# The MLP on h times g_mlp with its norm's row factor applied to h around it, block 0's gate behind its MLP, and h of two blocks kept on chip

## The chip, the cores and the metric

The kernel runs on one core of one Trainium2 chip. The metric is the device time of one execution in microseconds (us). Five engines work side by side, each through its own instructions in order: TensorE (PE, matrix products; its weight loads are listed as PEld), VectorE (DVE), ScalarE (ACT), GpSimd (POOL) and SyncE (SP, whose queue issues all DMA transfers of this kernel). Tiles lie in on-chip memory (SBUF), 128 partitions wide; products land in PSUM.

## The reference

One step of a one-layer encoder over 2048 prompt frames and 32 frames of a second, cached stream, 2080 rows of 1024 channels. Cut to what the change touches:

```python
def rmsnorm(x, g, eps=EPS):
    y = x * lax.rsqrt(jnp.mean(x * x, axis=-1, keepdims=True) + eps)
    return y * g

hp = hp + merge(oa, ob, ...)            # attention outputs @ w_out, residual

def ffn_ple(h, p, g_mlp, w_up, w_down, w_ple_gate, w_ple_proj):
    c = rmsnorm(h, g_mlp)
    h = h + jnp.square(jax.nn.relu(c @ w_up)) @ w_down
    return h + jax.nn.sigmoid(h @ w_ple_gate) * (p @ w_ple_proj)

y = rmsnorm(hp, g_final)
```

w_up is 1024 x 4096, w_down 4096 x 1024, w_ple_gate 1024 x 1024, w_ple_proj 256 x 1024. Before the merge stand two attention groups, A (differential, over all earlier chunks) and B (a band).

With r the factor 1/sqrt(mean(h*h) + eps) of a row and v = 1/(r*r), a squared relu lets r*r be taken out: the square of relu(r * x) is r*r times the square of relu(x). So h + MLP(r*h*g) equals r*r * (h*v + MLP(h*g)). The kernel after computes it in this second form.

## The kernel before, in words

**Tiling.** Channels lie on the partitions and rows along the free axis. The 2080 rows are cut into four blocks of 512, 512, 512 and 544 (`BN`); block 3's products are made in two pieces of 272 (`SUBS`). Every float32 operand of a product is split into a rounded high part and the rest: ACT writes the high part, POOL or DVE subtracts it (`split`), and `mm3` makes three products per term: high x high, high x low, low x high. `wunit` loads 512 KB of weights (ring `wr` of two), ACT makes `wh` and POOL makes `wl` (rings of three).

**Order.** The program is written as stages, but a planner orders each engine's instructions: it runs the program on a timeline of its own and takes, of the instructions that are ready there, the one that stands earliest in the program. So a later stage fills the gaps of an earlier one. On the chip the order of each engine is then fixed, and an engine that waits holds everything behind it.

**The stages that matter here**, as `run` writes them: attention A of the late rows (`JA1`); outproj(0) and outproj(1) with the loads and norms of the attention outputs (`oload`); the MLP of block 0, alone, then of block 1, alone; gate(1) and final(1); then outproj(2), outproj(3), gate(0), the norms of blocks 2 and 3, and one MLP for both of them; gate(2), final(2), gate(3), final(3). `outproj` adds x to the product, collects the sum of squares of h on POOL (`sq`) and writes h to `hS` in device memory. `colnorm` sums `sq` over the partitions with two products by a matrix of ones and makes r with ACT and DVE, which goes to `rS`. `cnorm` reads h and r back, multiplies by g_mlp and r on DVE and splits the result into cH and cL. The MLP then reads h a second time (`hload`) and adds the down product of each chunk to it on DVE. `mlp` runs 16 chunks of 256 hidden channels; `mlp_up` of a chunk comes before `mlp_down` of the chunk before.

**Block 0's gate** comes late: its h is written back to `hS` after its MLP, and read again for gate(0) behind outproj(3).

**Rings and memory.** In the first part the MLPs and gate(1) share two PSUM buffers (`mm`, MM = 2), because attention holds the other six; afterwards these six become `md`, used by outproj(2), outproj(3), gate and the down products. `actq` has two buffers: a block's cH and cL, then gate's hH and hL. `hq` has one buffer for h, `uq` a ring of eight for the MLP's, gate's and final's working tiles. In the second part `acth` has four buffers and `hh` two. The pools `wk` and `fk` (working tiles: `tmp` a ring of four, `r` and `acc` of two) are opened twice, for the first and for the second part. A pool opened over freed memory waits, tile by tile, for those who used it.

The lines to know: L149 and L153 are `split`, L168 to L170 the three products of `mm3`, L838 to L844 outproj's add and squares, L859 cnorm's multiply, L880 to L890 the norm factor, L914 relu, L949 the add of a down product to h, L993 to L1014 the gate, L1031 to L1054 final.

## Time and profile before

| | us |
|---|---|
| median of 3 runs | 3315.77 |
| lowest, highest | 3314.72, 3323.53 |
| the profiled execution | 3310.69 |
| its span, first to last instruction | 3308.8 |
| TensorE busy | 3096.1 |
| mean granted TensorE clock | 0.975 |

Where the stages lie in the profiled execution, from the first and last starts of their tiles: outproj(0) begins at 932.5; the MLPs of blocks 0 and 1 run from 1073 to 2154, beside attention, whose last row goes out at 2210; gate(1) starts at 2154; outproj(2) and (3) lie between 2219 and 2339; gate(0) between 2339 and 2405; the MLP of blocks 2 and 3 from 2406 to 3165; then the last two gates.

How to read it: a page gives the busy time of each engine, then groups of instructions by source line, with `out<-in` by the names of the tiles, a count, busy time and mean time of one. An idle stretch of an engine is put down to what ended it. Matmuls are pipelined: each is listed with its own length, but the next starts before it ends, so the distance from start to start is what a matmul costs. A busy-time table by stretch gives for each engine the busy us and, in brackets, the instructions.

### The profile page before, as it was taken

What the parts mean: (1) busy time and instruction counts of PE and PEld (TensorE: products, weight loads), DVE (VectorE), ACT (ScalarE), POOL (GpSimd) and SP (SyncE); (2) the same over time, 40 slices, a digit from 0 to 9 for tenths busy, and PEclk for the clock granted to TensorE, in tenths of its full rate; (3) what the DMA queues carried; (4) which work ended last, traced back from release to release, by engine and by line L of the source; (5) the groups of instructions that cost most, each with busy time, mean ns of one, the idle gap of its engine ahead of it and who ended that gap; (6) DMA issues with size and microseconds to landing.
All of it is one profiled execution on the core that took longest, in us unless ns stands there. A gap on an engine that the chain in (4) does not pass through costs nothing. (4 is left out here: it accounts for less than half of the span.)

```text
span 3308.8 us, 50118 instructions
## 1 busy us (share of the span) xinstructions
PE 3096.1 (94%) x17881; PEld 2710.5 (82%) x17881; DVE 1669.4 (50%) x3952; ACT 1698.4 (51%) x3717; POOL 1468.8 (44%) x1083
## 2 busy tenths in 40 slices
PE   6988989999989999999899999989889999999998
PEld 6877778889977888777777877877779999999987
DVE  6117777454555545476765656656442232223335
ACT  4226666566665766666665656654442222222245
POOL 4335654432334433444544444565753333333365
PEclk9999899999999999999999999999999999999999
DMA  7488777686788654545655345347631111111123
GB/s 232 159 252 244 205 217 205 204 247 195 215 235 215 180 145 134 155 132 138 200 136 136 112 132 144 116 146 226 178 105 52 45 46 50 46 45 45 53 86 101
DMA packets 519073, 488.93 MB, mean 148 GB/s; under 512 B 37884, under 2 KB 414016, under 8 KB 518824
## 3 DMA queue, kind: packets, MB, share of 16 engines
q1 hardware_dynamic: 518824, 485.73, 50.8%
q8 instruction: 142, 2.33, 0.3%
q14 instruction: 107, 0.88, 0.1%
HBM read 379.06 MB, written 110.49 MB: 148 GB/s over the span
## 5 line engine op out<-in xcount | busy, mean ns | idle before, releaser
L153 POOL TENSOR_TENSOR wl<-wr,wh 128x1024 fp32r<-128x1024 f32 x338 | 820.0, 2427 | 1026.3 <-ACT wh L149 983.4
L949 DVE TENSOR_TENSOR h<-h,dps 128x512 f32<-128x512 f32 (+1 forms) x640 | 373.1, 585 | 584.6 <-PE dps L170 572.2
L149 ACT ACTIVATE wh<-wr 128x1024 fp32r<-128x1024 f32 x338 | 356.9, 1056 | 563.9 <-PE dps L169 278.4
L168 PE MATMUL dps<-uh,wh 128*128 128x512 f32 (+1 forms) x1280 | 459.7, 359 | 22.0 <-DVE h L949 16.7
L168 PE MATMUL ups<-cH,wh 128*128 128x512 f32 (+1 forms) x1280 | 452.0, 353 | 8.2 <-ACT relu L914 8.0
L170 PE MATMUL dps<-uh,wl 128*128 128x512 f32 (+1 forms) x1280 | 451.7, 353 | 0.0
L169 PE MATMUL ups<-cL,wh 128*128 128x512 f32 (+1 forms) x1280 | 451.5, 353 | 0.0
L169 PE MATMUL dps<-ul,wh 128*128 128x512 f32 (+1 forms) x1280 | 451.4, 353 | 0.0
L170 PE MATMUL ups<-cH,wl 128*128 128x512 f32 (+1 forms) x1280 | 451.0, 352 | 0.0
L168 PEld LDWEIGHTS dps<-uh,wh 128*128 128x128 f32 x1280 | 242.8, 190 | 57.0 <-DVE h L949 22.8
L168 PEld LDWEIGHTS ups<-cH,wh 128*128 128x128 f32 x1280 | 241.4, 189 | 40.9 <-ACT relu L914 8.6
L170 PEld LDWEIGHTS dps<-uh,wl 128*128 128x128 f32 x1280 | 241.7, 189 | 33.0
L169 PEld LDWEIGHTS ups<-cL,wh 128*128 128x128 f32 x1280 | 241.9, 189 | 31.1 <-DVE cL L153 0.4
L170 PEld LDWEIGHTS ups<-cH,wl 128*128 128x128 f32 x1280 | 241.7, 189 | 30.1
L153 POOL TENSOR_TENSOR ul<-relu,uh 128x272 fp32r<-128x272 f32 (+1 forms) x160 | 174.9, 1093 | 205.2 <-ACT uh L149 203.8
L169 PEld LDWEIGHTS dps<-ul,wh 128*128 128x128 f32 x1280 | 242.4, 189 | 26.3
L168 PE MATMUL qps<-aH,wh 128*128 128x512 f32 (+1 forms) x640 | 231.5, 362 | 6.8 <-ACT wh L149 3.4
L545 PE MATMUL s<-ka,q 128*128 128x256 f32 (+4 forms) x784 | 192.7, 348 | 40.8 <-issue 15.7
L169 PE MATMUL qps<-aL,wh 128*128 128x512 f32 (+1 forms) x640 | 229.8, 359 | 0.0
L170 PE MATMUL qps<-aH,wl 128*128 128x512 f32 (+1 forms) x640 | 229.3, 358 | 0.0
L559 ACT ACTIVATE e<-s,nm 128x512 f32<-128x512 f32 (+3 forms) x256 | 155.1, 610 | 94.7 <-DVE nm L551 70.9
L545 PEld LDWEIGHTS s<-ka,q 128*128 128x128 f32 (+1 forms) x784 | 135.7, 195 | 66.4 <-issue 27.9
(217 smaller groups left out, 7056.9 us busy)
## 6 DMA issues: line engine op xcount, KB each, us to landing
wr<-w_up SPq DMA_DIRECT2D x96, 512.0 KB, 4.2
wr<-w_down SPq DMA_DIRECT2D x96, 512.0 KB, 3.7
wr<-w_in SPq DMA_DIRECT2D x74, 512.0 KB, 5.2
q<-qS SPq DMA_DIRECT2D x256, 128.0 KB, 4.3
v<-vSa SPq DMA_DIRECT2D x64, 512.0 KB, 3.8
ka<-kS SPq DMA_DIRECT2D x32, 512.0 KB, 7.9
wr<-w_out SPq DMA_DIRECT2D x32, 512.0 KB, 5.0
wr<-w_ple_gate SPq DMA_DIRECT2D x32, 512.0 KB, 4.4
```

What stands on the lines that cost most here:

```text
L149: nc.scalar.activation(hi, raw, AF.Copy)
L153: eng.tensor_tensor(lo, raw, hi.bitcast(F32), op=ALU.subtract)
L168: nc.tensor.matmul(ps, lh, rh, start=start and i == 0, stop=False)
L169: nc.tensor.matmul(ps, lh, rl, start=False, stop=False)
L170: nc.tensor.matmul(ps, ll, rh, start=False, stop=stop and i == n - 1)
L545: nc.tensor.matmul(s, q[:, m, hl, P * qi : P * qi + nr], kt[:, m, k0 : k0 + n], start=hl == 0, stop=hl == 1)
L559: nc.scalar.activation(dst, src, AF.Exp, bias=nmx, accum_out=z[:nr, m, bi : bi + 1])
L949: nc.vector.tensor_tensor(hv, hv, ps, op=ALU.add)
```

## The change

Four things, in the order of the program.

1. The norm's factor no longer goes into the MLP's input. `split_g` makes cH and cL from h in two instructions: ACT scales by g_mlp while it rounds, DVE multiplies by g_mlp and subtracts. `msnorm` takes the place of `colnorm`: it makes v (the mean square plus EPS) and 1/v, and writes both to device memory (`vS[2]`, `rS`). `mlp` loads v behind its first up chunk and POOL multiplies h by it, eight instructions per block; in the last down chunk each add to h is followed by a DVE multiply by 1/v.
2. gate and final of block 0 come right behind its MLP, as those of block 1 did; block 0's h is no longer written back and read again, and gate(0) and final(0) are gone from the second part.
3. Of blocks 2 and 3 h is made in place: both tiles of `hh` exist before outproj(2), outproj reads x into them and adds there, and h is not written to `hS`. Block 2's cH and cL are made inside outproj(2); block 3's (`csplit`) behind outproj(3). The MLP takes the tiles as they are.
4. `wk` and `fk` are opened once, ahead of the attention of the late rows, and stay.

```diff
-        self.vS = [self.dram([KC, D], F32, "vSa"), self.dram([KC, D], F32, "vSb")]
+        self.vS = [self.dram([KC, D], F32, "vSa"), self.dram([KC, D], F32, "vSb"), self.dram([P, T], F32, "vSm")]
...
+    def split_g(self, k, src, n, c):
+        nc = self.nc
+        g = self.g_mlp[:, k : k + 1]
+        hi, lo = c[0][:, k, :n], c[1][:, k, :n]
+        nc.scalar.activation(hi, src, AF.Copy, scale=g)
+        nc.vector.scalar_tensor_tensor(lo, src, g, hi.bitcast(F32), op0=ALU.mult, op1=ALU.subtract)
...
-            h = wk.tile([P, BLK], F32, tag="tmp", bufs=4, name="hd")[:, :n]
+            if hfull is None:
+                h = wk.tile([P, BLK], F32, tag="tmp", bufs=4, name="hd")[:, :n]
+            else:
+                h = hfull[:, d, :n]
             self.dma(h, self.xT[:, d, t0 : t0 + n])
...
-            self.dma(self.hS[:, d, t0 : t0 + n], h)
+            if hfull is None:
+                self.dma(self.hS[:, d, t0 : t0 + n], h)
+            if c is not None:
+                self.split_g(d, h, n, c)
             yield
 
-    def cnorm(self, b, wk, act, out):
+    def csplit(self, b, wk, act, out, hfull=None):
...
-        r = wk.tile([P, BLK], F32, tag="r", bufs=2, name="rl")[:, :n]
-        self.dma(r, self.rS[:, t0 : t0 + n])
         for k in range(8):
-            tmp = wk.tile([P, BLK], F32, tag="tmp", bufs=4, name="tmp")[:, :n]
-            self.dma(tmp, self.hS[:, k, t0 : t0 + n])
-            nc.vector.scalar_tensor_tensor(
-                tmp, tmp, self.g_mlp[:, k : k + 1], r, op0=ALU.mult, op1=ALU.mult
-            )
-            self.split(cH[:, k, :n], cL[:, k, :n], tmp, "act", "dve" if k % 2 else "pool")
+            if hfull is None:
+                tmp = wk.tile([P, BLK], F32, tag="tmp", bufs=4, name="tmp")[:, :n]
+                self.dma(tmp, self.hS[:, k, t0 : t0 + n])
+            else:
+                tmp = hfull[:, k, :n]
+            self.split_g(k, tmp, n, (cH, cL))
             yield
...
+    def msnorm(self, sq, b, wk, ps):
...
+            nc.scalar.activation(v, ss, AF.Copy, scale=1.0 / D, bias=EPS)
+            nc.scalar.activation(y, v, AF.Ln)
+            nc.scalar.activation(y, y, AF.Exp, scale=-1.0)
+            nc.vector.tensor_tensor(z, v, y, op=ALU.mult)
+            nc.vector.tensor_scalar(z, z, -1.0, 2.0, op0=ALU.mult, op1=ALU.add)
+            nc.vector.tensor_tensor(y, y, z, op=ALU.mult)
+        self.dma(self.vS[2][:, t0 : t0 + n], sq)
+        self.dma(self.rS[:, t0 : t0 + n], r)
...
+    def hscale(self, blocks, st, wk, src, name):
+        out = {}
+        for b in blocks:
+            out[b] = wk.tile([P, BLK], F32, tag="r", bufs=2, name=name)
+            self.dma(out[b][:, : BN[b]], src[:, 512 * b : 512 * b + BN[b]])
+        return out
...
                         nc.vector.tensor_tensor(hv, hv, ps, op=ALU.add)
+                        if rt is not None:
+                            nc.vector.tensor_tensor(hv, hv, rt[b][:, s0 : s0 + sn], op=ALU.mult)
...
-            if prev is not None:
+            if prev is None:
+                vt = self.hscale(blocks, st, wk, self.vS[2], "vt")
+                for d in range(8):
+                    for b in blocks:
+                        hv = st[b][0][:, d, : BN[b]]
+                        nc.gpsimd.tensor_tensor(hv, hv, vt[b][:, : BN[b]], op=ALU.mult)
+            else:
                 self.mlp_down(ch - 1, nf, blocks, prev, st, wk, md)
             prev = us
-        self.mlp_down(ch, nf, blocks, prev, st, wk, md)
+        self.mlp_down(ch, nf, blocks, prev, st, wk, md, self.hscale(blocks, st, wk, self.rS, "rt"))
...
             s12.close()
             self.small = False
+            wk = opened(top, "wk", 1)
+            fk = opened(top, "fk", 1)
             sq_ = ExitStack()
...
                 if b == 1:
-                    drain(self.cnorm(1, wk, actq, cn))
+                    drain(self.csplit(1, wk, actq, cn))
...
-                if b == 0:
-                    self.dma(self.hS[:, :, 512 * b : 512 * b + 512], h)
-            drain(self.gate(1, h, uq, actq, mm))
-            drain(self.final(1, h, uq, fk, mm))
+                drain(self.gate(b, h, uq, actq, mm))
+                drain(self.final(b, h, uq, fk, mm))
...
-            weave(self.outproj(2, wk, oa[2], md, acc[2]), self.oload(3, wk, act, oa), 1, 0, OW)
-            g = self.outproj(3, wk, oa[3], md, acc[3])
+            hb = {b: hh.tile([P, 8, BLK], F32, tag="h", name="h") for b in HALVES[1]}
+            g = self.oload(3, wk, act, oa)
             next(g)
-            self.colnorm(acc[2][0], 2, 1.0 / D, wk, mm, "mm", self.rS)
+            cn[2] = [act.tile([P, 8, BLK], F32R, tag="act", name=n) for n in ("cH2", "cL2")]
+            weave(self.outproj(2, wk, oa[2], md, acc[2], hb[2], cn[2]), g, 1, 0, OW)
+            g = self.outproj(3, wk, oa[3], md, acc[3], hb[3])
+            next(g)
+            self.msnorm(acc[2][0], 2, wk, mm)
             drain(g)
-            h = hload(hh, BLK, 0)
-            g = self.gate(0, h, up, act, md)
-            next(g)
-            self.colnorm(acc[3][0], 3, 1.0 / D, wk, mm, "mm", self.rS)
-            drain(g)
-            for b in HALVES[1]:
-                drain(self.cnorm(b, wk, act, cn))
-            f = self.final(0, h, up, fk, mm)
-            st = {b: (hload(hh, BLK, b),) + cn[b] for b in HALVES[1]}
+            drain(self.csplit(3, wk, act, cn, hb[3]))
+            st = {b: (hb[b],) + tuple(cn[b]) for b in HALVES[1]}
             m = self.mlp(HALVES[1], st, wk, up, mm, md)
             next(m)
-            drain(f)
+            self.msnorm(acc[3][0], 3, wk, mm)
             drain(m)
```

More of the change, by code (lines that the diff above doesn't have):

```diff
@@ L853, in cnorm @@
         out[b] = (cH, cL)
-        r = wk.tile([P, BLK], F32, tag="r", bufs=2, name="rl")[:, :n]
-        self.dma(r, self.rS[:, t0 : t0 + n])
         for k in range(8):
-            tmp = wk.tile([P, BLK], F32, tag="tmp", bufs=4, name="tmp")[:, :n]
-            self.dma(tmp, self.hS[:, k, t0 : t0 + n])
-            nc.vector.scalar_tensor_tensor(
-                tmp, tmp, self.g_mlp[:, k : k + 1], r, op0=ALU.mult, op1=ALU.mult
-            )
-            self.split(cH[:, k, :n], cL[:, k, :n], tmp, "act", "dve" if k % 2 else "pool")
-            yield
-    def colnorm(self, *args):
-        out = []
-        drain(self.colnorm2(*args, out))
-        return out[0]
+            if hfull is None:
[4 more added lines that the diff above has]
+            self.split_g(k, tmp, n, (cH, cL))
+            yield
+    def msnorm(self, sq, b, wk, ps):
+        nc = self.nc
+        n, t0 = BN[b], 512 * b
+        sh = wk.tile([P, BLK], F32R, tag="sh", bufs=1, name="msh")[:, :n]
+        sl = wk.tile([P, BLK], F32R, tag="sl", bufs=1, name="msl")[:, :n]
+        self.split(sh, sl, sq, "act", "dve")
+        r = wk.tile([P, BLK], F32, tag="r", bufs=2, name="mr")[:, :n]
+        w = wk.tile([P, BLK], F32, tag="tmp", bufs=4, name="mw")[:, :n]
+        for s0, sn in SUBS[b]:
+            ss = ps.tile([P, 512], F32, tag="mm", name="mss")[:, :sn]
+            nc.tensor.matmul(ss, self.ones, sh[:, s0 : s0 + sn], start=True, stop=False)
+            nc.tensor.matmul(ss, self.ones, sl[:, s0 : s0 + sn], start=False, stop=True)
+            v = sq[:, s0 : s0 + sn]
+            y = r[:, s0 : s0 + sn]
+            z = w[:, s0 : s0 + sn]
+            nc.scalar.activation(v, ss, AF.Copy, scale=1.0 / D, bias=EPS)
[6 more added lines that the diff above has]
+        self.dma(self.rS[:, t0 : t0 + n], r)
     def colnorm2(self, sq, b, scale, wk, tp, tag, dst, out):
@@ L917, in mlp_up, with mlp_down @@
         return us
[L919 removed]
+    def hscale(self, blocks, st, wk, src, name):
[4 more added lines that the diff above has]
+        return out
+    def mlp_down(self, ch, nf, blocks, us, st, wk, mm, rt=None):
         nc = self.nc
@@ L1161, in run @@
                     self.attn_a(js, pool, ps_s, ps_t, ps_o)
-            wk = opened(sq_, "wk", 1)
-            fk = opened(sq_, "fk", 1)
             self.gfin(fk)
-            acc, cn, st = {}, {}, {}
+            cn, st = {}, {}
+            acc = {b: [] for b in range(4)}
             def norms(b, act, ps):
-                self.colnorm(acc[b][0], b, 1.0 / D, wk, ps, "mm", self.rS)
+                self.msnorm(acc[b][0], b, wk, ps)
                 yield
-                yield from self.cnorm(b, wk, act, cn)
-            acc = {b: [] for b in range(4)}
+                yield from self.csplit(b, wk, act, cn)
             with ExitStack() as x:
```

10 lines of the change are left out of this document (3 added, 7 removed).

## The prediction

> **What bounds the kernel now.** I read the page's busy shares first, then busy time by stretch, then TensorE's waits in the stretch that the change rewrites.
>
> ```profile
> span 3308.8 us, 50118 instructions
> PE 3096.1 (94%) x17881; PEld 2710.5 (82%) x17881; DVE 1669.4 (50%) x3952; ACT 1698.4 (51%) x3717; POOL 1468.8 (44%) x1083
> ```
>
> TensorE is the bound: at most 212.7 us of the span are free of matmuls, and the change neither adds nor removes matmul work (two `css` products per piece become two `mss`). So it can only win or lose stalls. Where they lie, from the view of busy time by stretch (us, then busy us and instructions of PE, PEld, DVE, ACT, POOL; granted clock; DMA share; GB/s):
>
> ```profile
> 1050.00:1600.00 550.00, 520.83 (x2707) 439.16 (x2706) 321.98 (x839) 348.11 (x746) 243.73 (x162) 0.99 0.56 152
> 1600.00:2150.00 550.00, 522.53 (x2662) 439.06 (x2661) 344.95 (x740) 341.78 (x801) 250.62 (x187) 0.99 0.50 138
> 2154.00:2225.00 71.00, 63.24 (x307) 50.85 (x308) 34.60 (x51) 37.97 (x71) 45.16 (x35) 1.00 0.39 119
> 2225.00:2460.00 235.00, 209.32 (x1128) 180.45 (x1127) 130.75 (x176) 108.13 (x201) 148.99 (x83) 0.94 0.58 180
> 1587.00:1613.00 26.00, 20.78 (x87) 16.52 (x88) 24.74 (x47) 13.50 (x34) 14.13 (x11) 0.93 0.38 103
> 3142.00:3166.00 24.00, 24.00 (x152) 21.91 (x151) 18.14 (x32) 11.93 (x18) 15.48 (x10) 1.00 0.26 83
> ```
>
> The first two stretches are attention A1 with the MLPs of blocks 0 and 1 filling in: 29 us dead each, 5%. The third is gate(1) with the end of attention: 7.8 dead of 71, 11%. The fourth is outproj(2), outproj(3), gate(0), the norms of blocks 2 and 3 and the first MLP chunk: 25.7 dead, clock 0.94. The last two are the last down chunk of block 0 and of blocks 2 and 3. The fourth stretch's waits:
>
> ```profile
> PE ups L168 <- ACT relu L914: 8.0, 1, 8.0
> PE gps L168 <- ACT wh L149: 7.5, 1, 7.5
> PE ops L168 <- DVE hd L838: 3.6, 3, 1.9
> PE ops L169 <- DVE oact L153: 2.0, 1, 2.0
> ...
> PE dps L168 <- ACT wh L149: 0.6, 1, 0.6
> ```
>
> The nine rows (the four left out: 1.2, 1.1, 0.9, 0.7) add to 25.6 us. Behind the long ones the clock falls (busy time by stretch again, 5 us each; first figure after the comma-separated length is PE busy, the clock is third from the end):
>
> ```profile
> 2285.00:2290.00 5.00, 4.07 (x18) 3.75 (x18) 2.38 (x3) 1.29 (x2) 5.00 (x3) 0.50 0.69 227
> 2290.00:2295.00 5.00, 4.22 (x23) 4.00 (x22) 1.56 (x3) 0.74 (x2) 2.50 (x2) 0.71 0.80 236
> 2375.00:2380.00 5.00, 4.71 (x15) 3.79 (x16) 5.00 (x6) 2.82 (x5) 3.77 (x3) 0.67 0.59 173
> 2420.00:2425.00 5.00, 3.37 (x15) 3.38 (x16) 3.32 (x3) 2.38 (x4) 4.08 (x4) 0.50 0.02 5
> 2425.00:2430.00 5.00, 5.00 (x30) 4.61 (x30) 0.00 (x0) 2.29 (x6) 0.88 (x2) 0.89 0.00 0
> ```
>
> Busy time times the missing clock: 2.0 + 1.2 + 1.6 + 1.7 + 0.6 = 7.1 us. So 32.7 us is all that the transition can give back.
>
> **The change part by part.** Durations for all terms (groups by shape: count, then busy us and mean ns; below them matmuls in order of time, start and length):
>
> ```profile
> L949 DVE TENSOR_TENSOR h<-h,dps 128x512 f32<-128x512 f32 x384 | 261.9, 683 | 535.9 <-PE dps L170 534.1
> L949 DVE TENSOR_TENSOR h<-h,dps 128x272 f32<-128x272 f32 x256 | 111.5, 438 | 48.6 <-PE dps L170 38.1 <-DMA h<-hS 2.8
> L859 DVE SCALAR_TENSOR_TENSOR tmp<-tmp,g_mlp_s,rl 128x512 f32<-128x512 f32 x24 | 26.9, 1138 | 21.5 <-DMA tmp<-hS 20.9 <-issue 0.6
> L859 DVE SCALAR_TENSOR_TENSOR tmp<-tmp,g_mlp_s,rl 128x544 f32<-128x544 f32 x8 | 15.8, 2023 | 0.5 <-DMA tmp<-hS 0.5
> L153 DVE TENSOR_TENSOR hL<-h,hH 128x512 fp32r<-128x512 f32 x12 | 13.9, 1173 | 1.8 <-ACT hH L149 1.8
> L1014 POOL TENSOR_TENSOR h<-h,sig 128x512 f32<-128x512 f32 x24 | 33.2, 1384 | 25.4 <-DVE sig L1012 25.4
> ```
>
> ```profile
> 3165.45 0.28 PE L170 MATMUL dps<-uh,wl 128*128 128x272 f32 x1
> 3165.57 0.40 PE L168 MATMUL gps<-hH,wh 128*128 128x512 f32 x1
> 3165.80 0.40 PE L169 MATMUL gps<-hL,wh 128*128 128x512 f32 x1
> ```
>
> A matmul of 512 columns starts 0.23 us before the next, one of 272 some 0.125.
>
> (a) Transition, norms and gate(0) gone from it: -32.7. Outproj(2) and (3) write their h straight into `hb`, so the `hd` ring and its DMA round trip (3.6) go, gate(0)'s 7.5 goes, and cnorm's eight multiplies and eight splits per block become one ACT and one DVE instruction per k; block 2's run beside outproj(2). Late next: csplit(3). The pool `acth` has four buffers; oact(3) holds two and cn[2] two, so cH and cL of block 3 wait for outproj(3)'s last matmul. Then eight DVE instructions of the kind of L859; I take its 1.138 (the 512 row, mostly beside POOL work; 2.023 is the row of one crowded stretch): 9.1 us against the 24 matmuls of block 2 that stand first (5.5 at 0.23): 3.6 exposed, bounds 0 and 10.7 (8 x 2.023 - 5.5). Half clock after it: 1.5, near the 1.6 above. Oload(3) still waits for final(1)'s reads of h (their memory overlaps), so I keep the 2.0 of `oact`. On ACT block 2's splits wait for the same memory and the weight splits queue behind them; two units are loaded ahead, so 0, and without that one column, 5.5. (a) = -32.7 + 7.1 = -25.6.
>
> (b) POOL multiplies h by v (variance plus EPS): 8 for block 0, 8 for block 1, 16 for blocks 2 and 3. The first 16 lie where POOL is busy 44% (243.73 of 550): 0, by that cover. The last 16 take 22 us at 1.384, after msnorm(3) and a write and read of `vSm`; their cover is the second up chunk (2 x 24 x 0.23 plus 2 x 48 x 0.125, 23 us), which POOL shares with its own splits. Down chunk 0 then needs one d each 2.9 us. I take 1; without the cover 9. On SP the load of v waits for msnorm's write, and weight loads queue behind; again two are ahead.
>
> (c) The factor r at the end: each DVE add of the last down chunk gets a multiply behind it on the in-order engine, and the add's PSUM buffer waits behind both. Blocks 2 and 3: 8 x (0.683 + 2 x 0.438) = 12.5 us on DVE, in 24 us in which it already works 18.14: 6.6 too much. An add reads PSUM and never takes long; a multiply of two SBUF tiles can be held while POOL works:
>
> ```profile
> 3155.31 2.41 POOL L153 TENSOR_TENSOR wl<-wr,wh 128x1024 fp32r<-128x1024 f32 x1 [0.97 <-ACT wh L149]
> 3156.23 2.07 DVE L153 TENSOR_TENSOR hL<-h,hH 128x544 fp32r<-128x544 f32 x1
> 3166.12 0.74 DVE L153 TENSOR_TENSOR hL<-h,hH 128x512 fp32r<-128x512 f32 x1
> ```
>
> The second ends 0.6 us after the first, 2.07 for 0.7 us of work. POOL has 10 instructions there; I let each cost DVE 0.7: 7. Slack: gate(2) starts at 3165.57 and needs the last hL 21 matmuls on, 3170.4; it is there at 3166.9: 3.5. (c) = 6.6 + 7 - 3.5 + 1.5 of half clock = 11.6; bounds 3 (12.5 less DVE's idle 5.9 and the slack) and 20. The Trainium skill, SBUF — State Buffer, section SBUF: two separate sides, calls this an exclusive lock: a DVE instruction with two SBUF inputs and a GpSimd one that reads SBUF block each other for the whole instruction; the two rows agree, and its full price is a rival below.
>
> (d) Gate(0) and final(0) move between the MLPs of blocks 0 and 1, on the two-buffer `mm` ring, beside attention. Chunk 15 of block 0: DVE is at 24.74 of 26 there, but cnorm(1) leaves (8 x 1.138 plus 4 splits) and 8 multiplies and 4 hL splits come (5.5 + 4.7): 0. The gate itself: the wait before gate(1), 1.5; and the stretch of gate(1) is 11% dead against 5%, 4 us. Then csplit(1): cH and cL need hH's and hL's buffers (`actq` has two), so 8 x 1.138 = 9.1 us, formerly under the MLP, leave only gate(0)'s last products and final(0)'s transposes, 5 us, as filler: 4. h of block 1 (2 MB, one buffer, free after final(0)) comes under two up chunks: 0. (d) = 9.5; bounds 3 and 27. Also moved on SP's queue: ten weight loads, four of `pS`, eight outputs; DMA there is half busy: 0, by that cover.
>
> In order of time, the waits at gate(1), the first and last copy of final(1), and a load of h from issue to landing:
>
> ```profile
> 2154.25 0.47 PE L168 MATMUL gps<-hH,wh 128*128 128x512 f32 x1 [1.54 <-DVE h L949]
> 2223.05 0.50 PE L168 MATMUL gps<-hH,wh 128*128 128x512 f32 x1 [3.09 <-DVE sm L994]
> 2236.06 0.69 DVE L1036 COPY yn<-yp 128x512 f32<-128x512 f32 x1 [0.52 <-PE yp L1031]
> 2265.89 0.68 DVE L1036 COPY yn<-yp 128x512 f32<-128x512 f32 x1
> DMA to landing us min/median/max: 9.0/10.5/12.2
> ```
>
> (e) Gate(1) slides behind the end of attention by the 59 us put ahead of it (240 matmuls at 0.23, 32 transposes), so nothing covers its waits; one alone was 3.09. Eight columns at 1, its start 1.5, and block 1's last chunk with oload(2) on the same DVE, 4: 13.5 against the 7.8 dead before. (e) = +6; bounds 0 and 15.
>
> Fewer DMAs (block 0's h written and read again, 16 writes and 18 reads of `hS`): 0, TensorE waits for none of them above.
>
> Sum: -25.6 + 1 + 11.6 + 9.5 + 6 = +2.5. Against the profiled execution (3310.69, span 3308.8 and 1.9 around it) 3313.2; the median of the runs stands 5.1 above that execution, so 3318 us.
>
> On the clock a page disagrees with a row. Here the matmuls after one 2.25 us gap already stand 0.43 apart where 0.23 is usual:
>
> ```profile
> 1588.97 0.50 PE L168 MATMUL dps<-uh,wh 128*128 128x512 f32 x1 [2.25 <-DVE h L949]
> 1590.16 0.63 PE L169 MATMUL dps<-ul,wh 128*128 128x512 f32 x1
> 1590.59 0.63 PE L170 MATMUL dps<-uh,wl 128*128 128x512 f32 x1
> ```
>
> The Trainium skill, TensorE: Matmul & The Clock Gate, section What's actually happening, asks for an idle window of about 3.4 us before the rate halves; by it the two 1.5 us of half clock would fall away and the sum be -0.5, 3315. I go by the row.
>
> **The rivals.** Faster: the transition's gain stands and the new work hides. For it: DVE has 5.9 us free in the last chunk, and attention's matmuls wait behind filler and could use a gap. Against it: DVE at 24.74 of 26. With (c) 3, (d) 3, (e) 2: -25.6 + 9 = -16.6, 3299.
>
> Slower, the middle breaks: final(1) took 30 us (2236.06 to 2265.89), and h then 10.5; the ring `uq` of eight makes MLP 1's up chunk 1 wait for final(0)'s outputs as well. Cover is csplit(1)'s 9 and two up chunks: 22 us of matmuls, some 34 at the MLP's share of TensorE (its 1536 take 353 us of the 541 from 1613 to 2154, 0.65). So it decides where final(0) takes over 32 us. If it takes 60 beside attention, where DVE is 63% busy, 27 are uncovered at 0.65 each: 17.5 more, 3336. For it: one buffer for h; against: fill was 95% all along.
>
> Slower by the lock: if each POOL instruction of the last chunk holds DVE for its whole length, 15.48 us come in place of 7: (c) = 20, 3327. For it: the 2.07 row; against it: DVE may be amid an add, which goes on. The Trainium skill's page SBUF — State Buffer would have it so, with its lock for the whole instruction.
>
> The wait only moves: csplit(3) at 2.023 each exposes 10.7 in place of 3.6, 3325. For it: POOL splits weights there; against: half the DVE work is gone.
>
> **How the numbers follow.** Forecast 0.32 (own range 3308 to 3329), faster 0.30, the middle 0.17, the lock 0.13, the moved wait 0.08. About 0.3% (10 us) is what a measurement here tells from no change. Faster by more than that: 0.28 of the faster rival and 0.02 of the forecast, 0.30. Slower: 0.16 + 0.10 + 0.06 of the three slow rivals and 0.08 of the forecast, 0.40. Within: 0.30. The range 3288 to 3344 takes in the faster rival's lower half and the middle's price with room, and leaves 2 in 10 out.
>
> **What would show it.** Right: no TensorE wait over 4 us between the end of attention and the MLP of blocks 2 and 3; DVE over 95% busy in the last down chunk and a TensorE wait on DVE before gate(2); gate(1) after attention's last transposes. Wrong: gate(2) starting without a wait ((c) too dear), stretches of attention more than 7% dead around gate(0) ((d) too cheap), or an 8 us wait at the first `ups` ((a) too good).

## The result, and the profile after

The changed kernel takes 3334.99 us (median of 5 runs, 3331.9 to 3339.59); the kernel before took 3314.72 beside it (5 runs). The ratio is 1.0063, with a 95% interval of 1.0042 to 1.0084: slower by 0.6%, some 20 us. The profiled execution took 3339.59, 28.9 more than that of before. The prediction's range, 3288 to 3344, holds the time; its forecast of 3318 is 17 too low, and the time lies outside the forecast's own range, 3308 to 3329.

The head of the page of the changed kernel:

```profile
span 3337.7 us, 50074 instructions
...
PE 3123.8 (94%) x17881; PEld 2718.6 (81%) x17881; DVE 1684.0 (50%) x3971; ACT 1702.3 (51%) x3717; POOL 1483.3 (44%) x1099
```

TensorE does the same 17881 matmuls and is free of them for 213.9 us, against 212.7 before. So the loss isn't more idle time: the same matmuls count for 27.7 us more. Busy time runs from a matmul's start to its end, so that one at half clock, or one that stands alone among waits, counts for more than the 0.23 us after which the next could start. Where that happens shows in busy time by stretch (length, then busy us and instructions of PE, PEld, DVE, ACT, POOL; granted clock; DMA share; GB/s):

```profile
1600.00:2150.00 550.00, 508.93 (x2514) 421.83 (x2513) 356.84 (x754) 344.99 (x810) 258.60 (x194) 0.96 0.49 135
1582.90:1624.10 41.20, 34.31 (x163) 28.01 (x162) 33.62 (x73) 24.43 (x60) 21.20 (x15) 0.92 0.71 187
1624.10:1746.00 121.90, 107.19 (x531) 88.21 (x530) 89.97 (x195) 91.36 (x224) 61.73 (x47) 0.92 0.50 135
1700.00:1800.00 100.00, 87.06 (x418) 71.47 (x419) 73.67 (x159) 69.17 (x175) 50.76 (x38) 0.90 0.52 154
1715.00:1746.00 31.00, 21.77 (x91) 16.42 (x90) 29.27 (x74) 27.77 (x77) 11.56 (x10) 0.74 0.46 138
1746.00:2248.50 502.50, 476.16 (x2345) 394.18 (x2344) 298.74 (x602) 289.61 (x654) 234.52 (x173) 0.98 0.47 134
2205.00:2276.00 71.00, 62.39 (x257) 47.86 (x256) 42.63 (x49) 26.70 (x42) 38.46 (x27) 0.98 0.62 201
2248.50:2275.90 27.40, 23.67 (x98) 17.52 (x96) 19.65 (x24) 9.75 (x14) 16.05 (x8) 1.00 0.54 173
2276.00:2343.00 67.00, 59.64 (x239) 45.33 (x240) 15.85 (x19) 27.50 (x40) 40.86 (x24) 0.97 0.25 71
2343.00:2448.00 105.00, 99.76 (x614) 90.40 (x613) 58.43 (x85) 47.26 (x85) 63.08 (x32) 0.97 0.41 124
3170.00:3195.00 25.00, 22.58 (x136) 19.49 (x135) 24.90 (x39) 7.80 (x12) 13.53 (x8) 1.00 0.18 51
```

The first row is the one to read. In the same 550 us that held 2662 matmuls before, 2514 now run: 148 fewer, at 550 / 2662 = 0.21 us each some 30 us of work. It is 13.6 us less busy time and 0.03 less clock on 509 to 522 us (16). The next rows go through that stretch: the last down chunk of block 0 (1582.9 to 1624.1, where gate(0) starts); gate(0) and final(0), up to MLP 1's first product at 1746; within these the 100 us around final(0), and 1715 to 1746, the time between the last product of gate(0) and the first of MLP 1, filled by attention and by final(0); then MLP 1 up to its last down chunk. The rows from 2205 on are the end of MLP 1, its last down chunk by itself, and gate(1), no longer covered by attention; then outproj(2) and outproj(3); the last is the end of the last down chunk of blocks 2 and 3, with DVE at 24.90 of 25.

The last down chunk of block 0 looks bad, but it took as long in the kernel before (its row there):

```profile
1571.70:1612.50 40.80, 33.99 (x165) 28.00 (x164) 37.89 (x64) 23.87 (x56) 22.82 (x15) 0.96 0.49 143
```

MLP 1's stretch loses as well, though the change puts nothing into it but eight multiplies by v on POOL: 2345 matmuls take 502.5 us. Before, the 507.5 us behind block 0's last down chunk held 2469 (1612.5 to 2120); at that pace 2345 take 482, an estimate, since the mix of matmuls isn't quite the same.

From the last product of the last down chunk of blocks 2 and 3 to the end both profiled executions take 143.3 us (3165.45 to 3308.8, 3194.4 to 3337.7), so nothing was lost there.

TensorE's waits over the whole span:

```profile
PE s L545 <- DMA ka<-kS: 26.8, 8, 5.2
...
PE dps L168 <- DVE h L985: 16.6, 17, 2.7
PE s L545 <- ACT e L559: 13.4, 10, 3.4
PE tpp L617 <- DVE e L582: 11.9, 9, 2.3
...
PE ops L168 <- DVE h L848: 4.8, 1, 4.8
```

The 8.0 before the first `ups` and gate(0)'s 7.5 are gone, as the prediction had it. In their place attention's own waits stand longer: for its keys (`ka`, 11.0 before, 26.8 now), for its exponentials (7.7, 13.4) and for the weights made of them (`e` of L582; 7.5, 11.9). Such a wait shows only where TensorE's order has too few products of an MLP ahead of the one that waits.

Two places in order of time, the end of block 0's last down chunk and final(0) (start, length; a wait stands in brackets):

```profile
1613.49 2.69 PE L545 MATMUL s<-ka,q 128*128 128x512 f32 x6 [5.25 <-DMA ka<-kS]
1615.97 0.63 PE L168 MATMUL dps<-uh,wh 128*128 128x512 f32 x1
...
1624.07 0.40 PE L168 MATMUL gps<-hH,wh 128*128 128x512 f32 x1
...
1718.00 0.65 PE L1076 MATMUL yp<-ident,h 128*128 128x128 f32 x4
...
1726.08 2.16 PE L545 MATMUL s<-ka,q 128*128 128x512 f32 x4 [1.59 <-ACT e L559]
...
1741.58 0.66 PE L1076 MATMUL yp<-ident,h 128*128 128x128 f32 x4 [0.25 <-ACT junk L1083]
1744.41 1.97 PE L617 MATMUL tpp<-ident,e 128*128 128x128 f32 x8 [2.18 <-DVE e L582]
1746.04 0.78 PE L168 MATMUL ups<-cH,wh 128*128 128x512 f32 x1
1746.61 0.63 PE L169 MATMUL ups<-cL,wh 128*128 128x512 f32 x1
1747.04 0.63 PE L170 MATMUL ups<-cH,wl 128*128 128x512 f32 x1
```

At 1613 the keys of attention's next group are not there. Eighteen down products of MLP 0 are still to come (1615.97 to 1624), but they stand behind attention's scores in TensorE's order, and gate(0), which needs the whole of h, behind them. From 1718 to 1742 final(0) sends its eight tiles (`yp`) through the two buffers of `mm`, among attention's scores; MLP 1's first product stands behind all of them, at 1746, and starts at half clock, 0.43 apart.

### The profile page after: what moved, and what is told of

It reads as the page before. It is cut to its first block, busy times and chain, and to the rows that moved or that the text cites. A ratio compares the mean times of both kernels' runs of the same rounds, so it can differ in the third digit from the quotient of the medians.

```text
span 3337.7 us, 50074 instructions
## 1 busy us (share of the span) xinstructions
PE 3123.8 (94%) x17881; PEld 2718.6 (81%) x17881; DVE 1684.0 (50%) x3971; ACT 1702.3 (51%) x3717; POOL 1483.3 (44%) x1099
## 4 chain that ended last, share of the span: by engine, by line
PE 41%; DVE 5%; ACT 2%; DMA 2%; issue 1%; POOL 1%; SPq 0%; DVEq 0%; POOLq 0%; ACTq 0%
PE ups L168 5%; PE ups L170 5%; PE ups L169 5%; PE dps L168 5%; PE dps L169 5%; PE dps L170 5%; PE gps L168 1%; PE s L545 1%; PE gps L169 1%; PE gps L170 1%; DVE e L582 1%; DMA ka<-kS 1%; PE ops L170 1%; PE ops L169 1%; PE ops L168 1%
## 5 line engine op out<-in xcount | busy, mean ns | idle before, releaser
L168 PE MATMUL dps<-uh,wh 128*128 128x512 f32 (+1 forms) x1280 | 460.6, 360 | 21.9 <-DVE h L985 16.6
L169 PEld LDWEIGHTS dps<-ul,wh 128*128 128x128 f32 x1280 | 243.0, 190 | 27.7
L545 PE MATMUL s<-ka,q 128*128 128x256 f32 (+4 forms) x784 | 198.1, 357 | 54.2 <-DMA ka<-kS 26.8
```

Source lines behind the costliest of these rows:

```text
L168: nc.tensor.matmul(ps, lh, rh, start=start and i == 0, stop=False)
L169: nc.tensor.matmul(ps, lh, rl, start=False, stop=False)
L545: nc.tensor.matmul(s, q[:, m, hl, P * qi : P * qi + nr], kt[:, m, k0 : k0 + n], start=hl == 0, stop=hl == 1)
```

## The experiments

Each run was timed beside the kernel before, on several chips, on which that kernel took 3303 to 3315; so only ratios are compared, and "under" and "over" are in us on 3315, from the ratios. The changed kernel stands at 1.0063, 21 over the kernel before.

| kernel | ratio (95% interval) | us against before |
|---|---|---|
| changed kernel | 1.0063 (1.0042 to 1.0084) | +21 |
| gate0_last | 1.0043 (1.0029 to 1.0057) | +14 |
| no_final0 | 0.9987 (0.9977 to 0.9997) | -4 |
| no_r23 | 1.0077 (1.0060 to 1.0093) | +26 |
| ups_first | 1.0537 (1.0516 to 1.0558) | +178 |
| final0_late | 1.0048 (1.0032 to 1.0064) | +16 |
| gate1_md | 1.0033 (1.0021 to 1.0045) | +11 |
| final0_late_md | 1.0029 (1.0019 to 1.0039) | +10 |
| ups_first2 | 1.0060 (1.0046 to 1.0074) | +20 |
| final0_spread_md | 0.9957 (0.9942 to 0.9972) | -14 |
| no_v23 | 1.0074 (1.0054 to 1.0094) | +25 |
| no_r01 | 1.0007 (0.9992 to 1.0022) | +2 |
| spread_md_pool | 1.0066 (1.0053 to 1.0078) | +22 |

An edit can make the planner order the whole program anew, so it must be asked how far a run still has the changed kernel's order. In no_v23 TensorE runs the same instructions in the same order from first to last, in no_r23 up to 3199 us, in gate1_md up to 2268. At 1.0074 and 1.0077, inside the changed kernel's interval, the first two show how well one order repeats. The other runs leave that order at 1590 (gate0_last), 1613 (no_r01; spread_md_pool too) or 1718. What a new order by itself is worth no run measures, and their differences hold it.

### Final(0) left out

```diff
                 drain(self.gate(b, h, uq, actq, mm))
-                drain(self.final(b, h, uq, fk, mm))
+                if b == 1:
+                    drain(self.final(b, h, uq, fk, mm))
```

> Leaves out final(0), so the first 512 rows of y are not written; gate(0) stays in the middle. Theory A1 (the first up product of MLP 1 stands behind final(0)'s eight transposed tiles in the two-buffer PSUM ring, and these wait for a DVE and ACT full of attention): of the 21 us lost between 1715 and 1746 only the wait for csplit(1), done at 1726, stays: 12 to 17 less, and 2 for the transposes themselves: 3316 to 3322. Rival A2 (csplit(1) is what MLP 1 waits for): at most 6 less, 3329 or more.

Measured 0.9987: 25 us under the changed kernel. Busy time by stretch of this kernel:

```profile
1600.00:2150.00 550.00, 517.63 (x2592) 429.04 (x2591) 353.93 (x724) 345.25 (x802) 272.43 (x203) 0.98 0.50 135
1622.80:1717.10 94.30, 87.03 (x450) 72.78 (x448) 63.67 (x127) 66.64 (x153) 51.20 (x38) 0.98 0.53 138
1717.10:2220.00 502.90, 481.68 (x2413) 398.96 (x2414) 306.56 (x632) 305.16 (x699) 246.88 (x185) 0.99 0.47 132
```

78 of the 148 missing matmuls are back, and MLP 1's first product starts at 1717.1 in place of 1746. csplit(1) is still there, so it isn't csplit(1) that MLP 1 waited for: its eight columns come from 1712 to 1726, and the products, which take them one by one, start at 1717 without a wait for them.

12 to 17 were expected and 25 came. From gate(0)'s first product to MLP 1's first (second row), free time and missing clock are 7.3 and 1.7 us (0.02 of 87.03); in the changed kernel they are 14.7 and 8.6 (0.08 of 107.19). That is 14 less, as expected. The rest lies behind it: MLP 1 up to its last down chunk (third row) runs 68 matmuls more than the changed kernel does in the same time, some 14 us. Nothing was left out there, and how much of that is final(0)'s doing and how much the new order's is not shown. The wait for keys before 1613 stands in this kernel too (5.96), so it is no part of the gain.

### MLP 1's first up chunk ahead of final(0)

```diff
+                    s1 = [None] + list(cn[1])
+                    m = self.mlp((1,), {1: s1}, wk, uq, mm, mm)
+                    next(m)
+                    drain(self.final(0, h, fq, fk, mm))
                 h = hload(hq, 512, b)
```

> The middle stays, but MLP 1's first up chunk (48 products, 11 us) is issued between csplit(1) and final(0), so its products take the PSUM ring before final(0)'s tiles; final gets working tiles of its own, four buffers. Nothing is left out. Theory A1 (order in the PSUM ring): the 11 us of products fill the gap, 8 to 11 less: 3324 to 3327. Rival A2 (csplit(1) is what the products wait for): no gain, 3332 or more.

Measured 1.0537, which neither theory gives. MLP 1 ran its first chunk at 1716 and no other product until 2060:

```profile
1750.00:2050.00 300.00, 192.37 (x903) 150.42 (x901) 189.25 (x488) 181.14 (x505) 43.81 (x75) 0.74 0.39 102
```

Attention alone keeps TensorE busy for 192 of 300 us at a clock of 0.74. The suspect is the new pool for final's working tiles, whose memory attention's tiles had used: the first of these tiles, `yn`, is written at 2030.8, though the transposes that it is copied from stand at 1732.75. The same order with the old ring of tiles:

```diff
-            fq = opened(sq_, "fq", 4)
...
-                    drain(self.final(0, h, fq, fk, mm))
+                    drain(self.final(0, h, uq, fk, mm))
```

> As ups_first (MLP 1's first up chunk issued between csplit(1) and final(0)), but final(0) and final(1) take their working tiles from the ring they had, not from a new pool. In ups_first MLP 1 stood still from 1737 to 2058, until attention's last scores. If the new pool's memory did that (it lies where attention's tiles lay, and waits tile by tile for them), the stop is gone here and the 48 products come ahead of final(0)'s tiles: 0 to 10 under the changed kernel, ratio to the kernel before 1.003 to 1.006. If the order itself did it (final(0) or h of block 1 behind products that wait for attention), the stop of 300 us stays: 1.05.

Measured 1.0060. The stop is gone, so the pool made it (that it was the place of its memory is the likely reading, and not shown by itself). And this order gained nothing that can be told. This kernel's row for 1700 to 1800 against the one above:

```profile
1700.00:1800.00 100.00, 83.20 (x411) 67.01 (x409) 76.40 (x164) 67.86 (x175) 42.99 (x33) 0.93 0.55 157
```

411 matmuls against 418: the 48 products run first, and the gap of 30 us then stands behind them, ahead of the second chunk. Theory A1 in this form, that 11 us of products would fill the gap, is wrong. What is left of it is that final(0)'s eight tiles, wherever they stand in this stretch, hold the products behind them. A place ahead of them in the PSUM ring doesn't help, so the ring's order alone isn't the cause.

### Final(0) beside the MLP of blocks 2 and 3

```diff
+                if b == 0:
+                    self.dma(self.hS[:, :, :512], h)
+                else:
+                    drain(self.final(b, h, uq, fk, mm))
...
             self.msnorm(acc[3][0], 3, wk, mm)
+            drain(self.final(0, None, up, fk, mm))
             drain(m)
```

> Gate(0) stays in the middle and its h goes to device memory; final(0) runs beside the first chunk of the MLP of blocks 2 and 3, fed in pieces of 128 rows by four channel tiles from device memory into that MLP's working tiles. Nothing is left out. Theory A1 (final(0)'s tiles in the two-buffer PSUM ring hold MLP 1's first products): as without final(0), 25 us under the changed kernel, less the transposes' 2 to 3 us: 20 to 23 under it, ratio to the kernel before 0.999 to 1.001. Rival (final(0) costs what it costs wherever it stands, since TensorE's order is full): within 8 us of the changed kernel, ratio 1.004 or more.

Measured 1.0048, 5 under the changed kernel, which the two intervals don't tell apart. From 1600 to 2150 TensorE runs 2596 matmuls, as many as without final(0), but the loss is back 700 us later. TensorE's waits from 2430 to 2485, then DVE there in order of time, and POOL beside it:

```profile
PE dps L168 <- DVE h L985: 6.7, 2, 5.1
PE yp L1081 <- DMA hp<-hS: 5.7, 2, 3.1
```

```profile
2449.07 1.28 DVE L1120 TENSOR_TENSOR fst<-fst 128x1 f32<-128x1 f32 x1 [0.75 <-ACT junk L1088]
2451.98 1.26 DVE L180 TENSOR_TENSOR rsv<-rsv,rsy 128x1 f32<-128x1 f32 x1
2453.28 0.15 DVE L181 TENSOR_SCALAR rsv<-rsv 128x1 f32<-128x1 f32 x1
2453.47 1.06 DVE L182 TENSOR_TENSOR rsy<-rsy,rsv 128x1 f32<-128x1 f32 x1
...
2455.05 3.03 DVE L1104 SCALAR_TENSOR_TENSOR yn<-yn,rsy,gf 128x512 f32<-128x512 f32 x2
...
2463.09 0.15 DVE L180 TENSOR_TENSOR rsv<-rsv,rsy 128x1 f32<-128x1 f32 x1
```

```profile
2445.15 5.18 POOL L1001 TENSOR_TENSOR h<-h,vt 128x512 f32<-128x512 f32 x4
2450.60 9.99 POOL L1001 TENSOR_TENSOR h<-h,vt 128x544 f32<-128x544 f32 x7 [0.27 <-DMA vt<-vSm]
```

final(0) has come beside the change's own multiplies of h by v on POOL. DVE's instructions on one column with two inputs take 1.06 to 1.28 us each there, and the two scalings of `yn` 3.03. The same instruction takes 0.15 at 2463.09, when POOL has ended its multiplies at 2461.9 and does nothing. DVE is in order, so the adds of `dps` stand behind all this, and TensorE waits 5.1 us for one. Nearly as much, 5.7, it waits for pieces of h that final(0) must now read back (`hp`). Neither theory named either; the two say that the price depends on what stands beside final(0), and on where its h lies.

### Gate(1) on six PSUM buffers

```diff
+                if b == 1:
+                    psx.close()
+                    md = opened(top, "md", 8 - MM, PSUM, "right")
-                drain(self.gate(b, h, uq, actq, mm))
+                drain(self.gate(b, h, uq, actq, md if b else mm))
```

> The six PSUM buffers that attention leaves are opened ahead of gate(1), and gate(1) uses them in place of the ring of two. Nothing is left out. Theory C (term (e): gate(1) alone waits 0.81 us in each of its columns for the min that empties its two-buffer ring, 6.6 us in all): 5 to 8 less than the changed kernel, ratio to the kernel before 1.004 to 1.005. Rival (the waits are DVE's own chain and only move to the next reader): within 2 us of the changed kernel, 1.0057 or more.

Measured 1.0033, 10 under the changed kernel. Up to 2268, in the last down chunk of MLP 1, TensorE's order is the changed kernel's, so the gain lies behind it. Gate(1) of this kernel:

```profile
2258.00:2321.00 63.00, 62.13 (x268) 49.34 (x267) 22.23 (x27) 29.39 (x43) 47.44 (x27) 1.00 0.29 86
```

0.9 us free in 63, against 7.4 in 67: the waits for `sm` are gone. The measured 10 is a little over the 5 to 8 expected.

> Both together, and the last down chunk of MLP 1 too uses the six buffers. Nothing is left out. If the two causes are separate their gains add, and the last chunk's waits for its adds (some 5 us) shrink: 21 + 6 + 3 = 30 under the changed kernel, ratio to the kernel before 0.997 (0.995 to 0.999), faster than both. If only the first holds: 0.999 to 1.001.

This is final0_late and gate1_md together, and MLP 1's last down chunk on the six buffers as well. Measured 1.0029: no more than gate1_md alone. The gains don't add, because final(0) brings its loss to the new place: from 2340 to 2480 TensorE again waits 6.7 us for adds and 5.7 for `hp`, and outproj(3)'s waits are 4 us longer than in the changed kernel.

### Both causes out of the way

```diff
-            drain(self.final(0, None, up, fk, mm))
+            next(m)
+            next(m)
+            f = self.final(0, None, Spare(wk), fk, md)
+            for _ in range(4):
+                next(m)
+                next(f)
+                next(m)
+            drain(f)
             drain(m)
```

> As gate1_md, and final(0) leaves the middle for the MLP of blocks 2 and 3, one piece of 128 rows behind every second chunk from the third on, transposed through the six-buffer ring, with working tiles that this MLP leaves unused. Nothing is left out. Theory A1 (final(0)'s price is the order of the ring in which its tiles stand ahead of the next products, so it is small where six buffers and idle DVE and ACT take it): the 17 to 20 us of the middle go and do not come back; 10 + 17 = 27 under the changed kernel, ratio to the kernel before 0.997 to 0.999. Rival (32 transposes with their evictions cost some 17 us of TensorE wherever they stand in a full TensorE order, as beside the first chunk in final0_late): 1.002 to 1.004.

Measured 0.9957 (0.9942 to 0.9972): 14 us under the kernel before and 35 under the changed kernel, more than expected, and as much as no_final0 (25) and gate1_md (10) together. Busy time by stretch: the attention stretch, and the part of the MLP in which the four pieces of final(0) run:

```profile
1600.00:2150.00 550.00, 517.10 (x2600) 429.23 (x2599) 354.33 (x732) 346.84 (x804) 273.86 (x204) 0.98 0.51 140
2500.00:2850.00 350.00, 350.00 (x2183) 317.92 (x2182) 115.05 (x225) 97.30 (x184) 111.30 (x74) 1.00 0.19 58
```

In the last row TensorE isn't free for a moment: with DVE a third busy and six buffers, final(0) costs its transposes and nothing else. So the rival, that 32 transposes cost 17 us wherever they stand, is out. Whether the six buffers or the idle DVE does it, these runs don't tell apart.

### Gate(0) and final(0) at the very end

```diff
+                if b == 0:
+                    self.dma(self.hS[:, :, 512 * b : 512 * b + 512], h)
...
+            h0 = hload(hh, BLK, 0)
+            drain(g)
+            g = self.gate(0, h0, up, act, md)
+            f = self.final(3, st[3][0], up, fk, mm)
```

> Block 0's gate and final leave the middle: its h is written to device memory behind its MLP and read back at the very end, gate(0) follows gate(3), final(3) runs beside gate(0) and final(0) closes the kernel. Nothing is left out. Theory A (the middle is what was mis-sized): at equal matmul work the stretch from 1594 to 1761 us of the changed kernel holds 47 us of stalls and slow clock against 16 before; those 31 go, and the same 57 us of products come back at the end with 3 to 8 us of gate stalls: 3335 - 31 + 5 = about 3309, 3300 to 3314. By the prediction's own price of the middle (9.5) it would be 3335 - 9.5 + 5 = 3330. Rival B (the loss comes from the new order of loads and instructions all over the kernel, not from where gate(0) stands): 3328 or more.

Measured 1.0043, 7 under the changed kernel where theory A had 21 to 35 and the prediction's price of the middle 5. The attention stretch, and the end from the last down product on:

```profile
1600.00:2150.00 550.00, 520.76 (x2616) 432.30 (x2617) 349.78 (x725) 330.88 (x769) 253.47 (x187) 0.98 0.49 137
3104.00:3324.00 220.00, 190.10 (x1069) 162.72 (x1067) 120.01 (x185) 117.15 (x252) 140.94 (x98) 0.96 0.36 112
```

The middle is repaired to 2616 of 2662. But the end holds 29.9 us without a matmul, and takes 219.0 us from the last down product where the changed kernel took 143.3: 76 more for some 58 us of products (240 at 0.23, 32 transposes at about 0.1). So theory A was right on the place and wrong on what the same work costs at the end, some 17 us of stalls and not 3 to 8.

### The multiplies by v and by 1/v

```diff
-        self.mlp_down(ch, nf, blocks, prev, st, wk, md, self.hscale(blocks, st, wk, self.rS, "rt"))
+        rt = self.hscale(blocks, st, wk, self.rS, "rt") if len(blocks) == 1 else None
+        self.mlp_down(ch, nf, blocks, prev, st, wk, md, rt)
```

> Leaves out the multiply by 1/v in the last down chunk of blocks 2 and 3 (their MLP result stays v times too large). By the prediction's term (c), 11.6 us: 3323. By the trace of the changed kernel, where the last down chunk is 95% matmuls and the time from its last product to the end is 143.3 us as before: 0 to 3 less, 3332 to 3335.

Measured 1.0077: no gain, so term (c), 11.6 us, cost nothing that this run can tell (the two intervals leave room for a few us). Likewise the multiplies by v on POOL:

```diff
+                        if len(blocks) == 1:
                             nc.gpsimd.tensor_tensor(hv, hv, vt[b][:, : BN[b]], op=ALU.mult)
```

> Leaves out the multiply of h by v on POOL in the MLP of blocks 2 and 3 (their rows come out wrong). By the prediction's term (b): 1 us less than the changed kernel (at most 9). By the trace of the changed kernel, where the stretch 2447 to 2480 loses 1.4 us in all: 0 to 1 less.

Measured 1.0074, no gain, and here TensorE's order is the same throughout. The multiply by 1/v in the other two blocks is another matter (`len(blocks) == 2` in the first diff):

> Leaves out the multiply by 1/v in the last down chunk of blocks 0 and 1 (their rows come out wrong). The prediction counted it as nothing in block 0 and within 4 us in block 1. If it delays the start of gate(0) (10 us lost from 1605 to 1624, DVE full) and of gate(1): 5 to 10 less than the changed kernel, ratio to the kernel before 1.0035 to 1.005. If the starts wait for the keys of attention and for the chain of h, split and weights anyway: 0 to 3 less, 1.0055 or more.

Measured 1.0007: 18 us under the changed kernel. One of its TensorE waits over the span, and its stretches, which hold the same work as those of the changed kernel: the last down chunk of block 0, MLP 1 up to its last down chunk, and that chunk:

```profile
PE dps L168 <- DVE h L985: 6.9, 8, 2.0
```

```profile
1575.90:1613.60 37.70, 33.90 (x162) 27.77 (x161) 30.31 (x67) 25.02 (x60) 19.59 (x15) 0.95 0.78 204
1735.30:2217.80 482.50, 466.62 (x2343) 388.45 (x2343) 291.98 (x600) 285.54 (x652) 233.56 (x173) 0.99 0.47 132
2217.80:2242.40 24.60, 22.77 (x98) 18.02 (x97) 15.01 (x22) 10.59 (x15) 14.76 (x9) 1.00 0.96 328
```

The multiplies stand in the two last down chunks alone. These take 37.7 and 24.6 us in place of 41.2 and 27.4: 6 us are won where something was left out. The other 20 between these two executions lie in MLP 1's stretch, 482.5 us for 2343 matmuls in place of 502.5 for 2345, where no multiply by 1/v stands. So it is with the waits of down products for an add, which fall from 16.6 to 6.9 over the span: in the last down chunk of block 1 they fall by 2.4, and the rest lies in chunks that have no such multiply. The order is another from 1613 on, and which part of it makes MLP 1's stretch shorter these runs don't tell. The sixteen instructions on POOL in place of DVE, on top of final0_spread_md:

```diff
+                            eng = nc.gpsimd if len(blocks) == 1 else nc.vector
-                            nc.vector.tensor_tensor(hv, hv, rt[b][:, s0 : s0 + sn], op=ALU.mult)
+                            eng.tensor_tensor(hv, hv, rt[b][:, s0 : s0 + sn], op=ALU.mult)
```

> As final0_spread_md, and in the last down chunk of blocks 0 and 1 the multiply by 1/v is done by POOL, in blocks 2 and 3 by DVE as before. Nothing is left out. Without these 16 multiplies the changed kernel was some 18 us shorter (no_r01). Theory D (DVE, full with attention there, is what they cost): POOL, under half busy, takes them, and 6 to 14 us of the 18 come back: ratio to the kernel before 0.9915 to 0.994. Rival (a POOL multiply of 1.4 us holds DVE's multiplies and splits, and the split into hH and hL waits for it all the same): 0.995 or more, no gain over final0_spread_md.

Measured 1.0066, 36 over final0_spread_md. The rival said no gain; this is a loss, which neither theory gives. TensorE's two longest waits from 1590 to 1720 in this kernel:

```profile
PE s L556 <- ACT wh L160: 4.9, 1, 4.9
PE pps L179 <- DVE sig L1069: 4.0, 2, 3.1
```

No single wait carries it. Where the multiplies stand, POOL does what theory D said: block 0's last down chunk takes 37.6 us (1581.9 to 1619.5), as in no_r01. The loss comes behind it. Gate(0), to MLP 1's first product, takes 114.7 us where final0_spread_md takes 93.9, with 32 matmuls more in it, and MLP 1 up to its last down chunk runs 2362 matmuls in 507.3. TensorE's order is another from 1613 on. What in it costs the 36 us stays open; it shows that a small edit may move that much through the order.

## Why the prediction was in its range and wrong in its terms

**Right.** The bound: no matmul work came or went, and only stalls and clock moved. **Term (a)**, the transition: predicted to keep 7.1 us of 32.7. From 2343 to 2448 the changed kernel has 105 - 99.76 = 5.2 us free and 0.03 of clock on 99.76 (3.0): 8.2 kept. What is late next was misnamed: not csplit(3) but outproj(3)'s second product, 4.8 us behind the add into h, and there is no wait at the first `ups`. **Term (b)**: 1 predicted, 0 by no_v23. **Term (e)**, gate(1) uncovered: "eight columns at 1" are seven waits for `sm`, 6.6 in all and the longest 2.2; from 2205 to 2343 16.0 us are free against 7.8 before, +8.2 where +6 stood, inside the bounds of 0 and 15. Of its signs, three came: DVE at 24.90 of 25 in the last down chunk, waits of 2.1 us for its adds before gate(2), and gate(1) behind attention's last transposes. One came but for one wait of 4.8: none over 4 us between attention and the MLP of blocks 2 and 3. And one of its three signs of being wrong came: from 1600 to 2150 TensorE is free for 41 of 550 us, 7.5% where over 7% was to show that (d) was too cheap. (One reading of it was off by little: of the two stretches before, "29 us dead each", the second has 27.5.)

**Term (c) was sized at 11.6 and measured nothing in blocks 2 and 3.** The mechanism is there. By groups of the changed kernel:

```profile
L985 DVE TENSOR_TENSOR h<-h,dps 128x512 f32<-128x512 f32 x384 | 261.3, 683 | 549.3 <-PE dps L170 547.7
L985 DVE TENSOR_TENSOR h<-h,dps 128x272 f32<-128x272 f32 x256 | 111.4, 437 | 44.5 <-PE dps L170 36.9
...
L987 DVE TENSOR_TENSOR h<-h,rt 128x512 f32<-128x512 f32 x24 | 29.0, 1212 | 0.1
...
L987 DVE TENSOR_TENSOR h<-h,rt 128x272 f32<-128x272 f32 x16 | 13.8, 875 | 0.0
```

The multiply takes 1.21 us where the add, which reads PSUM, takes 0.68, and 0.88 where it takes 0.44. In blocks 2 and 3 alone the 24 of them take 9.2 and 14.0 us, 10.7 more than as many adds, where 7 were assumed for POOL's holding them. What failed is the step from "DVE full" to "TensorE waits". TensorE waited 2.1 us for adds and 0.6 at gate(2)'s start. Six PSUM buffers and 21 matmuls of slack lie between the two; that these took up the rest is the likely reading, and not tried.

**The same multiplies in blocks 0 and 1** the prediction had at 0 in block 0 (eight multiplies come where eight of cnorm(1) go) and within 4 us in block 1. Where they stand that is about right: leaving them out wins 3.5 and 2.8 us there, and block 0's last down chunk takes 41 us in both kernels. That the kernel without them is 18 us shorter comes for the most part from MLP 1's stretch and its other order, which the prediction gave no term.

**Term (d), the middle, was the large miss: 9.5 predicted, some 30 us measured**, over its upper bound of 27. Three of its parts can be compared. The gate's start, at 1.5, was not the trouble. csplit(1) was put at 4, with final(0)'s transposes counted as filler for it. It was the other way round: csplit(1) was ready at 1726, and final(0), to 1746, was what MLP 1's first product stood behind. From 1715 to 1746 9.2 us are free and 0.26 of clock is missing on 21.8 (5.7): 15 us, about half of the 30. And MLP 1's stretch, which the prediction took to run as before, takes some 20 us more than at the pace of before; this is about the other half. Part of it is gone without final(0) (no_final0) and all of it without the multiplies (no_r01), but both runs have a new order there, and what makes that half stays open.

**The rivals.** The time is that of "the middle breaks", 3336, and that rival rightly had final(0) beside attention as a cause. Its condition was wrong: it was to decide where final(0) takes over 32 us, through h's one buffer, at MLP 1's second up chunk. final(0) took 26, counted by its copies as final(1)'s 30 were (1718.8 to 1744.3), TensorE shows no wait for h, and the price was paid all the same, at MLP 1's first product and behind it. That its price fits the time, and that the range holds it, is in good part luck. The lock "at full price" is out by no_r23; its mechanism was seen, not its price. The faster rival is out by (d). The moved wait at csplit(3) did not come.

**The sum.** With the measured terms: -24.5 (a) + 0 (b) + 2.7 (c) + 30 (d) + 8.2 (e) = +16.4, against +20 in the medians and +28.9 between the two profiled executions.

## What to carry to other kernels

Of a stage that moves into a stretch with a full TensorE order, ask what stands behind it on TensorE and how fast DVE and ACT can empty its tiles there, not only for the sum of its instructions: final(0), 32 transposes, cost 25 us through two buffers beside attention, 20 through two buffers beside POOL's multiplies and with its h read back (1.0048 against 0.9987 without it), and nothing that shows where DVE was a third busy and six buffers stood ready. An engine at 99% need not cost anything: DVE at 24.90 of 25 cost nothing that could be told. Give a stage that leaves its cover the PSUM buffers that its cover leaves (10 us here), and spread what has no due time over the longest stretch that is otherwise even: the two together turned 21 us of loss into 14 of gain. And before a difference is put down to an edit, compare the order of TensorE's instructions and the length of stretches that hold the same matmuls: leaving out sixteen multiplies won 6 us where they stood and 20 where they did not.

## What the runs showed of the hardware that was not expected

A DVE instruction on a single column with two inputs in SBUF takes 0.15 us alone (2463.09) and up to 1.28 us beside POOL's multiplies of 1.3 to 1.4 us (5.18 / 4, 9.99 / 7), as the rows of final0_late show: the smallest instruction may take about as long as one of POOL's on 512 columns. The Trainium skill, SBUF — State Buffer, section SBUF: two separate sides, has the lock held for the whole of an instruction, whichever of the two comes first; the trace agrees, and the instruction with one input, 0.15 between them (2453.28), was not held. And idle time of TensorE was no measure of the loss: the changed kernel is free for 213.9 us against 212.7, and the loss lies in matmuls that ran one at a time or at a lower clock, 0.74 from 1715 to 1746.
